# First gated pair by plain products, one fixed order per round, later weight parts, and the squares' adds on VectorE

## The chip, the cores and the metric

The kernel runs on one core of one Trainium2 chip. The metric is the device time of one execution in microseconds. A core has TensorE (matrix products into PSUM), VectorE (DVE in the profile), ScalarE (ACT), GpSimd (POOL) and SyncE (SP, which here issues the loads). All engines run at once and wait for each other by semaphores.

## The reference: two layers of a hybrid decoder block

The input is 512 positions of width 1024, in float32. A layer adds, one after another:

```python
h = h + 0.5 * swiglu(rms_norm(h, ffn1_norm[l]), ffn1_w_gate[l], ffn1_w_up[l], ffn1_w_down[l])
h = h + hybrid_mixer(rms_norm(h, mix_norm[l]), w_in[l], ..., w_out[l])
h = h + 0.5 * swiglu(rms_norm(h, ffn2_norm[l]), ffn2_w_gate[l], ffn2_w_up[l], ffn2_w_down[l])
gate = jax.nn.sigmoid(rms_norm(h, ple_norm[l]) @ ple_w_gate[l])
h = h + gate * (p[l] @ ple_w_proj[l])
```

with `swiglu(x) = (silu(x @ w_gate) * (x @ w_up)) @ w_down` and 2816 hidden columns. `rms_norm` divides by the root of the mean square of a position and multiplies by a gain. The mixer has a recurrent group, a window attention and a gated delta rule side by side, then one output projection. A last `rms_norm` follows the two layers.

## The kernel before, in words

**Layout.** `hT` holds the state transposed: 8 tiles (k) of 128 channels x 512 positions. Every matrix product in float32 is done as three products of a high and a low half (`mm3`): high x high, high x low, low x high. A weight is split by ScalarE (high half, a copy into the rounded format) and VectorE (low half, raw minus high). The rms factor of a position is applied after the product, so the products need only `h` times the gain.

**A norm** (class `Norm`). As soon as a tile k of `hT` is final, `split` makes its high and low halves, and `square` adds its square to `acc` (ScalarE squares; POOL adds for k up to 6, VectorE for the last, L305). `sums` multiplies `acc` by ones on TensorE and takes the inverse root on VectorE (L320 to L334); `rows` spreads it over all partitions (L341, L343).

**A gated block** (`ffn`) has 11 pairs of a gate unit and an up unit ("g", "u"), each of 256 hidden columns, in two rounds of 5 and 6 pairs; behind each round comes its share of the down projection (`down`, tile `pd`). A unit's 1024 x 256 by 1024 x 512 product is done in seven block products (`Unit.p`, numbers 1 to 7) instead of eight, each 12 TensorE products of 256 columns: 84 a unit. For that the operand is combined in advance (`Norm.upper`, `Norm.lower`: differences of quarters of `h`, each split again), and so are the weights (`Weights`): parts a, b, c of 1024 elements and d of 512, two sums `s2` and `s4`, with one raw load summed by a POOL-issued DMA (`load2`, L408). The seven results are added up on VectorE (`c11`, `c21`, `c12`) after copies out of PSUM on ScalarE (L527, L532 `ys`, L536). `Gating` then scales, takes tanh and multiplies.

**Order.** TensorE keeps the order of the program. Other engines' instructions are ordered at compile time by a planner with a cost model, by the order of the program; inside `high_priority` they come ahead, and inside `manual_schedule` ScalarE and VectorE keep the written order among the instructions of that block. Before, a block's first pair (L599 to L650) and the units behind it (L655 to L734) are two such blocks; `taken` places `sums` and `rows` by a count of steps (AT0, AT1).

**Ahead.** `ffn` is a generator. While the stage before it runs, that stage calls `next(ahead)`: first the first raw loads, then part a of unit 0, part a of unit 1, then `s2`, `s4` and d of both and c of unit 0 (L571 to L590). The mixer calls it once ahead of its output projection and at its products n = 0, 2 and 4 (L1473); the embedding (`ple`) calls it at its start and three times behind `rows`, ahead of its gate products (L1508). For the first block of the program the main part calls it between the loads of x (L1567 to L1587). Raw weights share three buffers (tag `wr`).

Of the kernel before, what the change touches and what calls it, by code (L numbers as in the profile page):

```python
# [19 lines left out]
S = 512  # L20
# [23 lines left out]
AT0 = (9, 12)  # L44
# [18 lines left out]
def trunk(ctx: ExitStack, tc: tile.TileContext, a):  # L63
# [168 lines left out]
    class Norm:  # L232
# [32 lines left out]
        def plain(self, k, cs=ALL):  # L265
            x = self.x
            if k < 4:
# [30 lines left out]
        def square(self, k, t512, cs=ALL):  # L298
# [55 lines left out]
    def ffn(l, which, at=AT1):  # L354
        with ExitStack() as es:
# [38 lines left out]
            def load(u):  # L394
                j, m = units[u]
                src = a[f"{m}{which}"][l, j]
                if u not in raw1:
                    raw1[u] = loaded(src[:, 0:8], 8)
                    raw3[u] = wrp.tile([128, 8, 128], F32, tag="wr", name="wr")
# [108 lines left out]

            class Unit:
# [61 lines left out]
            if l + which > 1:  # L571
                for u in range(3):
                    load2(u)
            yield

            for u in range(2):
                load(u)
                load2(u)
                w = pipe[u] = Weights(u)
                w.part("a")  # L580
                yield
            for u in range(2):
                w = pipe[u]
# [3 lines left out]
                if u == 0:  # L587
                    w.part("c")
            load2(2)
# [4 lines left out]
            hs = [[ft.tile([128, 2, S], F32R, name=f"h{i}{c}") for c in "hl"] for i in range(2)]  # L594
            for r, (j0, j1) in enumerate(ROUNDS):
                us = list(range(2 * j0, 2 * j1))
                if r == 0:
                    load(2)
                    with tc.manual_schedule(engines=inner):  # L599
                        g, up = [Unit(*units[u], pipe.pop(u)) for u in us[0:2]]  # L600

                        for qs in (range(3), range(3, 4)):
                            for unit in (g, up):
                                unit.p(2, qs)
                        for i in range(2):
                            taken()
                        w = pipe[2] = Weights(2)
                        g.p(1)
                        taken()
                        g.w.part("b")  # L610
                        g.c11()
                        up.p(1)
                        taken()
                        up.w.part("b")
                        up.c11()
                        g.p(3)
# [1110 lines left out]
```

## Time and profile before

| | |
|---|---|
| time, median of 3 runs | 2096.07 us (2095.33 to 2098.78) |
| the profiled execution's own time | 2096.27 us |
| its span | 2094.3 us, 32231 instructions |
| TensorE busy | 1984.5 us, 12697 products |
| VectorE busy | 1575.2 us, 2578 instructions |
| ScalarE busy | 1000.6 us, 1648 instructions |
| POOL busy | 268.1 us, 254 instructions |
| moved by DMA | 256.08 MB |

A row of the profile names the source line (L305 is line 305), the engine, and out<-in by the program's tile names. Rows that group instructions give their number (x), busy time, mean length and the idle time of the engine ahead of them with what ended it. [...]

### The profile page before, as it was taken

Reading aid. Unit: us, or ns where it says so; the run is one execution under the profiler, and the core shown is the slowest. Engines: PE = TensorE matmul, PEld = TensorE weight load, DVE = VectorE, ACT = ScalarE, POOL = GpSimd, SP = SyncE. Lnnn points to the kernel's source line nnn. Section 1 sums busy time; section 2 is a strip of 40 time slices with the busy share of each in tenths; the row PEclk is TensorE's granted clock in tenths of the full one; section 3 lists DMA queues with packets and bytes.
Section 4 is the critical chain, followed back from the end, with each engine's and each line's share of the span. In section 5 each row is a group of like instructions: output and inputs, shape, how many; then the busy total and the mean of one; then the engine's idle time right before and its main releaser. Section 6 shows DMA issues by size and latency. Waiting matters only on the chain.

```text
span 2094.3 us, 32231 instructions
## 1 busy us (share of the span) xinstructions
PE 1984.5 (95%) x12697; PEld 1767.0 (84%) x12697; DVE 1575.2 (75%) x2578; ACT 1000.6 (48%) x1648; POOL 268.1 (13%) x254
## 2 busy tenths in 40 slices
PE   6999999999989999999979999999899899999997
PEld 5988998777669989997779899988676799899876
DVE  8975983879877857966779569757897888489466
ACT  5542652455645524543546336424365555156343
POOL 3000000152111000002100000010422100000012
PEclk8999999999999999999999999999999999999998
DMA  7763742211045735633337457322112367365411
GB/s 209 194 174 95 187 136 87 89 69 53 19 136 132 198 116 151 169 121 109 113 105 193 125 144 184 121 88 87 59 35 62 106 167 193 89 175 140 140 61 61
DMA packets 85991, 256.08 MB, mean 122 GB/s; under 512 B 9680, under 2 KB 17104, under 8 KB 85584
## 3 DMA queue, kind: packets, MB, share of 16 engines
q1 hardware_dynamic: 73168, 207.89, 31.2%
q0 software_dynamic: 12672, 46.14, 12.5%
q8 instruction: 99, 1.62, 0.3%
q14 instruction: 52, 0.43, 0.1%
HBM read 251.90 MB, written 2.10 MB: 121 GB/s over the span
## 4 chain that ended last, share of the span: by engine, by line
PE 72%; DVE 17%; ACT 4%; DMA 3%; issue 3%; SPq 0%; POOL 0%; DVEq 0%; ACTq 0%
PE pu L469 10%; PE pg L469 10%; PE qu L469 8%; PE qg L469 8%; PE pd L147 7%; PE pd L148 7%; PE pd L149 7%; DMA wr<-in_g_dram 2%; DMA wr<-in_d_dram 1%; PE pp L147 1%; DVE wl L124 1%; PE pp L148 1%; DVE X L252 1%; PE pp L149 1%; PE pwo L149 1%
## 5 line engine op out<-in xcount | busy, mean ns | idle before, releaser
L469 PE MATMUL pu<-T,gh 128*128 128x256 f32 x928 | 169.8, 281 | 0.0
L305 POOL TENSOR_TENSOR acc<-acc,sq 128x512 f32<-128x512 f32 (+1 forms) x55 | 85.5, 1554 | 587.0 <-ACT sq L304 495.0
L437 DVE TENSOR_TENSOR gl<-wr,gh 128x1024 fp32r<-128x1024 f32 x108 | 131.8, 1222 | 36.4 <-ACT gh L432 36.4
L469 PE MATMUL pg<-T,gh 128*128 128x256 f32 x768 | 143.7, 284 | 15.9 <-ACT T L251 7.3
L469 PEld LDWEIGHTS pu<-T,gh 128*128 128x128 f32 x928 | 143.4, 190 | 0.0
L147 PE MATMUL pd<-X,gh 128*128 128x512 f32 x352 | 138.1, 392 | 0.0
L148 PE MATMUL pd<-X,gh 128*128 128x512 f32 x352 | 137.9, 392 | 0.0
L149 PE MATMUL pd<-X,gl 128*128 128x512 f32 x352 | 137.5, 391 | 0.0
L469 PEld LDWEIGHTS pg<-T,gh 128*128 128x128 f32 x768 | 120.5, 192 | 17.7 <-ACT T L251 7.5
L469 PE MATMUL pu<-T,gl 128*128 128x256 f32 x464 | 131.1, 283 | 3.8 <-DVE gl L437 3.8
L129 DVE TENSOR_TENSOR gl<-wr,gh 128x1024 fp32r<-128x1024 f32 x52 | 63.6, 1223 | 94.3 <-ACT gh L128 94.3
L123 ACT ACTIVATE wh<-wr 128x1024 fp32r<-128x1024 f32 (+2 forms) x76 | 77.0, 1013 | 106.8 <-PE pp L148 48.4
L432 ACT ACTIVATE gh<-wr 128x1024 fp32r<-128x1024 f32 x108 | 111.2, 1045 | 28.4 <-PE pd L148 11.0
L469 PE MATMUL pg<-T,wh 128*128 128x256 f32 x640 | 116.8, 281 | 0.0
L128 ACT ACTIVATE gh<-wr 128x1024 fp32r<-128x1024 f32 x52 | 55.2, 1061 | 121.6 <-PE pd L148 95.7
L469 PE MATMUL pg<-T,gl 128*128 128x256 f32 x384 | 109.0, 284 | 1.6 <-DVE gl L437 1.6
L408 POOL DMA_DIRECT2D r<-in_u_dram x44 | 38.5, 875 | 556.9 <-DVE gl L437 179.4
L147 PE MATMUL pp<-X,wh 128*128 128x512 f32 x240 | 102.2, 426 | 0.0
L148 PE MATMUL pp<-X,wh 128*128 128x512 f32 x240 | 98.1, 409 | 3.9 <-DVE X L252 3.9
L437 DVE TENSOR_TENSOR wl<-wr,wh 128x1024 fp32r<-128x1024 f32 x68 | 83.1, 1222 | 24.5 <-ACT wh L432 24.5
L432 ACT ACTIVATE sh<-r 128x512 fp32r<-128x512 f32 x80 | 50.6, 632 | 105.0 <-DVE r L449 105.0
L469 PEld LDWEIGHTS pg<-T,wh 128*128 128x128 f32 x640 | 99.1, 190 | 0.3
(433 smaller groups left out, 6206.5 us busy)
## 6 DMA issues: line engine op xcount, KB each, us to landing
wr<-in_d_dram SPq DMA_DIRECT2D x64, 512.0 KB, 3.7
wr<-in_g_dram SPq DMA_DIRECT2D x44, 512.0 KB, 4.1
r<-in_g_dram SPq DMA_DIRECT2D x44, 512.0 KB, 3.8
wr<-in_u_dram SPq DMA_DIRECT2D x44, 512.0 KB, 3.7
r<-in_u_dram SPq DMA_DIRECT2D x44, 512.0 KB, 3.8
r<-in_g_dram POOLq DMA_DIRECT2D x44, 512.0 KB, 7.2
r<-in_u_dram POOLq DMA_DIRECT2D x44, 512.0 KB, 7.2
wr<-in_wi_dram SPq DMA_DIRECT2D x30, 512.0 KB, 3.3
```

The costliest lines, as they stand in the source:

```text
L123: A.activation(out=hi, in_=raw, func=AF.Copy)
L124: (via or V).tensor_tensor(out=lo, in0=raw, in1=hi.bitcast(F32), op=ALU.subtract)
L128: A.activation(out=hi, in_=x, func=AF.Copy)
L129: V.tensor_tensor(out=lo, in0=x, in1=hi.bitcast(F32), op=ALU.subtract)
L147: T.matmul(out=out, lhsT=wh, rhs=xh, start=start, stop=False)
L148: T.matmul(out=out, lhsT=wh, rhs=xl, start=False, stop=False)
L149: T.matmul(out=out, lhsT=wl, rhs=xh, start=False, stop=stop)
L305: (V if k == KD - 1 else G).tensor_tensor(out=acc, in0=acc, in1=sq, op=ALU.add)
L408: G.dma_start(out=r2.rearrange("p k n -> p (k n)"), in_=src[:, 8:16].rearrange("p k n -> p (k n)"), accum_op=ALU.add)
L432: A.activation(out=self.g[n][0], in_=self.of(n)[0], func=AF.Copy)
L437: V.tensor_tensor(out=g[1], in0=raw, in1=g[0].bitcast(F32), op=ALU.subtract)
L469: T.matmul(out=ps, lhsT=l_[:, q, :], rhs=r_, start=start and q == 0 and i == 0, stop=stop and q == 3 and i == 2, skip_group_check=more)
```

## The change

Seven edits. Only the first block of the program gets the plain pair; the other three blocks keep the seven products, with their orders and weight parts moved.

1. The first pair of the program is done by plain products: `firsts` are the four split raw weights, 24 `mm3` of 512 columns a unit, and the scaling is done from four banks (`PlainGating`). The splits of its norm, its squares and its sums move into that pair's order.
2. The first pair and the units behind it stand in one `manual_schedule` block, and so do the first two chunks of the down weights, in the round's last unit.
3. In the other blocks c of unit 0, and `s2`, `s4` and d of unit 1, are made in the first pair; the calls of `next(ahead)` come later.
4. The raw weights of the mixer's last four output products are loaded a product ahead.
5. The last four weights of the down projection are made ahead of the next norm.
6. Chunks of the down weights lose their high priority.
7. All adds of squares run on VectorE.

```diff
-                (V if k == KD - 1 else G).tensor_tensor(out=acc, in0=acc, in1=sq, op=ALU.add)
+                V.tensor_tensor(out=acc, in0=acc, in1=sq, op=ALU.add)
...
             def grouped(raw, k):
                 w = group(k, 128)
-                with tc.high_priority():
-                    split(raw, *w)
+                split(raw, *w)
...
+            class PlainGating(Gating):
...
+                def scale(self):
+                    self.cg = ft.tile([128, 2, S], F32, tag="cu", name="gs")
+                    for i in range(2):
+                        V.tensor_tensor(out=self.cg[:, i, :], in0=self.ps["g", i], in1=norm.rb, op=ALU.mult)
+                    self.th = ft.tile([128, 2, S], F32, tag="th", name="th")
...
-            if l + which > 1:
-                for u in range(3):
-                    load2(u)
-            yield
-            for u in range(2):
-                load(u)
-                load2(u)
-                w = pipe[u] = Weights(u)
-                w.part("a")
-                yield
-            for u in range(2):
-                w = pipe[u]
-                w.s2()
-                w.s4(0)
-                w.part("d")
-                if u == 0:
-                    w.part("c")
-            load2(2)
+            plain = l + which == 1
+            if plain:
+                raws = {}
+                for m in "gu":
+                    yield
+                    for b in (0, 8):
+                        raws[m, b] = loaded(a[f"{m}{which}"][l, 0][:, b:b + 8], 8)
+                yield
+                firsts = {k: grouped(raw, 8) for k, raw in raws.items()}
+                load(2)
+                load2(2)
+            else:
+                load2(0)
+                load2(1)
+                yield
+                load(0)
+                w = pipe[0] = Weights(0)
+                w.part("a")
+                yield
+                w.s2()
+                w.s4(0)
+                w.part("d")
+                yield
+                load(1)
+                w = pipe[1] = Weights(1)
+                w.part("a")
             yield
...
+            def first_pair():
+                load(2)
+                g, up = [Unit(*units[u], pipe.pop(u)) for u in us[0:2]]
...
+                g.p(1)
+                taken()
+                g.w.part("b")
+                load2(2)
+                g.c11()
+                g.w.part("c")
+                up.p(1)
+                taken()
+                up.w.s2()
+                up.w.s4(0)
+                up.c11()
+                up.w.part("d")
+                g.p(3)
+                taken()
+                g.p(7)
+                taken()
+                up.w.part("b")
...
+            def plain_pair():
+                ps = {}
+                for m in "gu":
+                    for i in range(2):
+                        o = ps[m, i] = bank([128, S], "p" + m)
+                        wh, wl = firsts[m, 8 * i]
+                        for n, (q, j) in enumerate((q, j) for q in range(4) for j in range(2)):
+                            b = 4 * (j if i else 1 - j) + q
+                            xh, xl = (x.both(0, 0, q), x.both(1, 0, q)) if j else (x.first[q][:, 0, :], x.first[q][:, 1, :])
+                            mm3(o, wh[:, b, :], wl[:, b, :], xh, xl, n == 0, n == 7)
+                    if m == "g":
+                        w = pipe[2] = Weights(2)
+                        for q in range(3):
+                            norm.plain(q)
+                            norm.upper(q, x.t512)
+                            norm.lower(q)
+                        for k in range(KD):
+                            norm.square(k, x.t512)
+                        w.part("a")
+                        w.s2()
+                norm.plain(3)
+                norm.upper(3, x.t512)
+                norm.lower(3)
+                norm.sums(t512)
+                w.part("b")
+                w.s4()
+                w.part("d")
+                w.part("c")
+                return None, None, PlainGating(ps, into(0, 0))
...
+                        else:
+                            raws = [loaded(src[l, d][:, t0:t0 + 8, :], 8) for d in range(2)]
                         unit.p(2)
...
                         if w:
                             w.s2()
                             w.lo("b")
+                        else:
+                            made[0] = grouped(raws[0], 8)
                         unit.p(1)
...
+            ws = []
+            for d in range(0, KD, 2):
+                raw = wrp.tile([128, KD, 128], F32, tag="wr", name="wr")
+                for i in range(2):
+                    nc.sync.dma_start(out=raw[:, 4 * i:4 * i + 4, :], in_=src[l, d + i][:, 18:22, :])
+                ws.append(grouped(raw, 8))
             nxt = Norm(gain, False)
...
             for n, d in enumerate(o):
-                if n in (0, 2, 4):
+                if n + 1 in range(4, KD):
+                    raws[n + 1] = wrp.tile([128, KD, 128], F32, tag="wr", name="wr")
+                    nc.sync.dma_start(out=raws[n + 1], in_=a["wo"][l, o[n + 1]])
+                if n == 6:
                     next(ahead)
...
                 nxt.add(d, d5)
+                if n in (3, 4):
+                    next(ahead)
...
             rb = norm.rows()
-            if ahead:
-                for i in range(3):
-                    next(ahead)
...
                     nxt.split(d, t512)
+                    if d in PAIRED[3:5]:
+                        next(ahead)
             ws = [weight(a["pg"][l, d], KD, 128) for d in range(last, KD)]
             if gain is not None:
+                next(ahead)
```

## Rows read from the trace of the kernel before

**Rows 1.** Stages: busy us (x count) of PE, PEld, DVE, ACT, POOL; clock, DMA, GB/s.

```profile
0.00:136.00 136.00, 113.33 (x864) 108.04 (x865) 115.67 (x164) 76.68 (x120) 23.09 (x23) 0.92 0.75 200
192.00:311.00 119.00, 118.60 (x1008) 118.40 (x1007) 101.47 (x125) 68.36 (x98) 6.93 (x8) 1.00 0.60 160
376.70:415.50 38.80, 36.85 (x156) 29.39 (x155) 32.60 (x78) 13.18 (x20) 4.49 (x4) 0.96 0.32 103
576.00:646.00 70.00, 62.50 (x301) 51.16 (x301) 50.93 (x84) 33.40 (x57) 13.45 (x11) 0.93 0.45 124
646.00:742.00 96.00, 91.46 (x754) 90.41 (x754) 81.98 (x110) 52.34 (x76) 6.95 (x9) 0.98 0.70 181
742.00:797.00 55.00, 55.00 (x242) 45.00 (x242) 29.44 (x36) 13.66 (x16) 0.86 (x1) 1.00 0.33 101
981.80:1004.00 22.20, 15.99 (x61) 12.55 (x59) 17.99 (x33) 10.99 (x19) 6.57 (x6) 0.85 0.79 203
1004.00:1050.00 46.00, 45.88 (x219) 38.37 (x218) 37.62 (x55) 23.89 (x40) 7.35 (x5) 0.96 0.29 97
1050.00:1072.00 22.00, 14.03 (x97) 13.53 (x95) 12.33 (x26) 8.75 (x19) 2.90 (x3) 0.77 0.28 72
...
2015.40:2031.30 15.90, 14.24 (x59) 11.33 (x58) 11.13 (x24) 7.56 (x13) 3.47 (x3) 0.89 0.20 65
```

**Rows 2.** Chain of waits, 60 to 80 us: start, length, what.

```profile
62.28 1.69 PE qg L469 x12
...
66.79 1.41 PE pg L469 x12
```

**Rows 3.** TensorE's waits, whole run: total us, times, longest.

```profile
PE pwo L149 <- DVE wl L124: 9.5, 6, 3.3
...
PE pg L469 <- ACT T L251: 7.3, 1, 7.3
...
PE qu L469 <- ACT ys L532: 6.9, 6, 1.9
PE ssc L318 <- DVE acc L305: 5.9, 3, 3.9
...
PE pwo L147 <- ACT wh L123: 5.4, 6, 1.4
```

**Rows 4.** Timeline of VectorE at 1053: start, length, instruction.

```profile
1053.77 2.40 DVE L287 SCALAR_TENSOR_TENSOR t<-hT,par,tg 128x256 f32<-128x256 f32 x1
```

**Rows 5.** Timeline of POOL at 1053.

```profile
1053.71 0.88 POOL L408 DMA_DIRECT2D r<-in_u_dram  x1 [6.38 <-ACT T L251]
1054.32 1.57 POOL L305 TENSOR_TENSOR acc<-acc,sq 128x512 f32<-128x512 f32 x1
```

**Rows 6.** VectorE's instructions by shape, 0 to 70 us: count, busy, mean ns.

```profile
L437 DVE TENSOR_TENSOR gl<-wr,gh 128x1024 fp32r<-128x1024 f32 x6 | 7.3, 1218 | 1.3 <-ACT gh L432 1.3
...
L294 DVE SCALAR_TENSOR_TENSOR t<-hT,neg,t 128x256 f32<-128x256 f32 x4 | 3.8, 952 | 0.0
...
L287 DVE SCALAR_TENSOR_TENSOR t<-hT,par,tg 128x256 f32<-128x256 f32 x4 | 1.9, 477 | 0.0
...
L305 DVE TENSOR_TENSOR acc<-acc,sq 128x512 f32<-128x512 f32 x1 | 0.7, 678 | 0.0
```

**Rows 7.** Timeline of POOL in the last stage.

```profile
2052.20 1.30 POOL L305 TENSOR_TENSOR acc<-acc,sq 128x512 f32<-128x512 f32 x1 [4.26 <-ACT sq L304]
```

**Rows 8.** ScalarE's instructions by shape, 0 to 70 us.

```profile
L128 ACT ACTIVATE T<-t 128x256 fp32r<-128x256 f32 x8 | 3.2, 403 | 2.1 <-DVE t L294 2.1
...
L128 ACT ACTIVATE T<-t 128x512 fp32r<-128x512 f32 x4 | 2.5, 623 | 2.2 <-DVE t L289 2.1
...
L276 ACT ACTIVATE tg<-hT,par 128x256 f32<-128x256 f32 x4 | 2.0, 493 | 0.0
```

**Rows 9.** Timeline of TensorE at 661.

```profile
661.24 0.39 PE L469 MATMUL qg<-T,sl 128*128 128x256 f32 x1 [1.92 <-DVE sl L437]
```

**Rows 10.** Timeline of ScalarE at 736.

```profile
736.47 1.06 ACT L128 ACTIVATE gh<-wr 128x1024 fp32r<-128x1024 f32 x1 [3.58 <-DMA wr<-in_d_dram]
```

More of the change, by code (lines that the diff above doesn't have):

```diff
@@ L266, in plain @@
             x = self.x
-            if k < 4:
+            if k < 4 and hasattr(x, "first"):
+                for i in range(2):
+                    A.activation(out=x(i, "B11", k), in_=x.first[k][:, i, H:S].bitcast(F32), func=AF.Copy)
+            elif k < 4:
                 self.gained(k, HALVES[1], x(0, "B11", k), x(1, "B11", k))
@@ L655, in ffn, with chunk @@
+                t0 = (0, 10)[r]
+                def chunk(d):
+                    if d not in made:
+                        made[d] = grouped(loaded(src[l, d][:, t0:t0 + 8, :], 8), 8)
+                    return made[d]
+                made = {}
                 with tc.manual_schedule(engines=inner):
+                    gate, last, pair, done = None, None, None, True
+                    if r == 0:
+                        gate, last, pair = plain_pair() if plain else first_pair()
+                        us = us[2:]
@@ L698, in ffn @@
                             w.lo("a")
+                        else:
+                            made[1] = grouped(raws[1], 8)
                         unit.p(3)
+                        if pair and not last:
+                            norm.rows()
                         unit.p(7)
@@ L705, in ffn @@
                         if pair:
+                            if not last:
+                                pair.scale()
+                                pair.tanh(0)
+                                pair.tanh(1)
+                                pair.silu()
                             pair.mult()
@@ L745, in end @@
                             ends[e] = halfgroup()
-                            with tc.high_priority():
-                                split(raw, *ends[e])
+                            split(raw, *ends[e])
                         i = 2 * (d % 2)
@@ L766, in ffn @@
                             pipe[2 * j1].whole()
-                        down(pds[d], v, range(8), range(8), True, False)
+                        down(pds[d], chunk(d), range(8), range(8), True, False)
                         if d == 0:
@@ L1571, in t512 @@
     def t512(n):
-        return per.tile([128, S], F32, tag=f"X{next(turn) % KD}", name=n)
-    for i in range(2):
-        load_x(PAIRED[4 * i:4 * i + 4])
-        for k in PAIRED[4 * i:4 * i + 4]:
-            norm.plain(k)
-        if i == 0:
+        return per.tile([128, S], F32, tag=f"X{4 + next(turn) % 4}", name=n)
+    norm.x.t512 = t512
+    norm.x.first = [wide(q) for q in range(4)]
+    load_x(PAIRED[0:2])
+    next(f)
+    load_x(PAIRED[2:8])
+    for q in range(4):
+        norm.gained(q, ALL, norm.x.first[q][:, 0, :], norm.x.first[q][:, 1, :])
+        norm.plain(q + 4)
+        if q == 0:
             next(f)
@@ L1581, in trunk @@
     load_rest()
-    for q in range(4):
-        norm.upper(q, t512)
-        norm.lower(q)
-    next(f)
-    for k in range(KD):
-        norm.square(k, t512)
     def rest(f, norm, gain):
```

123 lines of the change are left out of this document (55 added, 68 removed).

## The prediction

> **What bounds the kernel now.** I read the page's first part, where TensorE is busy nearly all of the span and VectorE comes next; so what can be won is TensorE's idle time and its time at the lower clock level. Then a table of stages [rows 1], which puts that in place; then who made TensorE wait; then single places. A product of 256 columns takes 1.41/12 = 0.1175 us at the full clock [rows 2], one of 512 takes 55.00/242 = 0.227 us (742 to 797, all TensorE [rows 1]). With these, TensorE's need against what each stretch of [rows 1] takes:
>
> (a) 0 to 136, the first round of the program: 10 units of 84 products, 840 x 0.1175 = 98.7 us. Lost: 37.
> (b) 576 to 646, the mixer's output projection and the first eight of the seven-product steps behind it: 192 x 0.227 + 96 x 0.1175 = 55 us, with about 1 for transposes 56. Lost: 14. The second layer has it again.
> (c) 981.8 to 1072, the per-layer embedding and the same eight steps: 240 x 0.227 + 11.3 + 1.5 (sums and rows) = 67.3 us of 90.2. Lost: 23.
> (d) 646 to 742, the rest of a first round: 744 x 0.1175 = 87.4 us of 96. Lost: 8.6, three times in all.
> (e) 376.7 to 415.5, the mixer's start: 1.95 us idle, and a clock of 0.96 that costs 1.6. Lost: 3.5, twice.
> (f) 2015.4 to 2031.3, the second embedding's start: 48 x 0.227 + 1.5 = 12.4 us. Lost: 3.5.
>
> Some 125 us in all. In the steady stretch 192 to 311 nothing is lost and VectorE is busy 101.47 of 119 us, 85% [rows 1]: it catches up 15% there and no more, so a boundary that leaves it late stays late for a while. The waits name it [rows 3]: the projection waits for low halves of weights (L124), the embedding's sums for the sum of squares (L305), the first step for the last split (L251). Two mechanisms lie behind that: weights of the next block are prepared ahead of what is wanted first, and POOL's adds lengthen VectorE's instructions. At 1053.77 an L287 of 128x256 takes 2.40 us beside a POOL add of 1.57 [rows 4, 5]; at the head its mean is 0.477 [rows 6]. That is 1.92 us on the chain that ends in TensorE's wait of 7.3 us [rows 3].
>
> **The squares.** 53 whole adds and two halves go from POOL to VectorE, at 0.678 us each there [rows 6]: 36 us, 4.1 for a norm's six. What comes back lies between 0 (the add at 2052.20 took 1.30 us [rows 7] in the last stage, where VectorE had nothing beside it) and 1.92 us an add (that L287). I take 1.0, nearer to the head, where four L294 average 0.952 against 0.477 [rows 6] and other lines lose too: 6 us a norm. So VectorE's load falls by some 2 us a norm, and the sum of squares no longer trails on an engine that takes 1.3 to 1.6 us an add. If nothing came back, VectorE would carry 36 us more (a rival below).
>
> [...]
>
> **(a) The head.** Before, TensorE runs without a break from 62.28 on; the third unit ends and the fourth begins at 63.97 [rows 2]. TensorE's new work is 96 x 0.227 = 21.8 us against 168 x 0.1175 = 19.7: 2.1 more, hidden as long as VectorE is the late one there. From VectorE go: the parts of two units (each three of 1.218, a half one of 0.68, two sums of 0.68: 5.7, together 11.4), the six sums of their products (3.0 by their sizes), one scaling (1.2), four low halves of B11 (1.9), POOL's lengthening (4). To it come: four low halves of plain weights (4.9), four of whole tiles (2.7), six adds (4.1), scaling and product from four separate banks (1.5) [rows 6]. Net: -21.5 + 13.2 = -8. Against it: the norm's splits and sums now stand inside the fixed order. In each of four rounds VectorE and ScalarE answer each other: ScalarE's 0.49, one of 0.48, high half 0.40, low 0.4, two of 0.48, high 0.62, low 0.68, one of 0.48, high 0.40, low 0.4, and part of the two copies of 0.40 [rows 6, 8]: near 5.8 us a round against 3.4 of VectorE's own work. That is 4 x 2.4 = 9.6 us of standing still at most, and none if the plain splits are placed between. I take 2, since most of those splits are ready then: -6. Ends: -12 (no standing still, every add worth 1.9) and +2. Its DMA is less, four loads of 512 KB instead of 2 x 1792 KB; but the fourth waits for one of three buffers, and in SP's queue behind it stand the third unit's loads and the constants that the norm's sums need. That costs nothing as long as the first plain split ends before TensorE's first 48 products do.
>
> **(b) The output projection.** The first weights' preparation moves from the products n = 0, 2, 4 to n = 3, 4, 6; the raw weights of n = 4 to 7 are loaded a product earlier; c of the first unit, and the sums and d of the second, move into the first pair. The third unit's second load now stands behind part b, whose end frees its buffer before too, so it starts no later. All of this stays inside the stretch, where VectorE is busy 50.93 of 70 us [rows 1]; the load changes by the squares alone, to 49 us, under TensorE's 56. What goes are the waits for L124 and its high halves (9.5 and 5.4 over both layers [rows 3]) and the lower clock behind them; what is late next is the norm's last split, since VectorE has 49 us of work in some 60. Of 14 lost I leave 8.5: -5.5 a layer, -11. Ends -18 and -3.
>
> **(c) The embedding.** In 981.8 to 1004 no weights of the next block are made any more ahead of the sums: 22.2 could become 48 x 0.227 + 1.5 = 12.4, and I take -9. They come in the 46 us of the gate's products instead: VectorE 37.62 [rows 1] + 4.5 (a, two sums, d, a) + 4.1 - 6 = 40 of 46 us, still covered; without that cover the 4.5 would be seen. At 1050 to 1072 the 7.3 us shrink by the 1.9 of that L287 and one queue place, and the clock of 0.77 [rows 1] recovers with them: -4. Sum -13, ends -18 and -5.
>
> **(d) First rounds.** The third unit's part d now stands ahead of the next unit's work; before, TensorE waited 1.92 us for it [rows 9]. The moved c and d can make VectorE up to 2.9 us later just before. I take -1, three times. At the round's end ScalarE stood 3.58 us before a high half whose load had not landed, and behind it the copy-out `ys` held TensorE [rows 10]; six such waits make 6.9 us [rows 3]. The two first chunks now have fixed places, the later ones are still placed by the planner: -2. Together -5, ends -10 and +4. A new wait: the chunk's high half on ScalarE waits for its weight buffer until the previous unit's p5 has run; behind it are c11 and `ys`, and p4 waits for `ys`. p3 and p7 (2.8 us) cover the 2.5 us of ScalarE between.
>
> **(e), (f) Ends of blocks.** No POOL add beside the last splits, and the four last weights made early: -2.5 for each mixer, -3 for the second embedding. Together -8, ends -10.5 and -1.
>
> **Sum.** -6 - 11 - 13 - 5 - 8 = -43 us against the profiled execution's own 2096.27 (its span 2094.3 and 2.0 around it), which is 0.2 above the median shown: 2053.
>
> **The rivals.**
> *Small gain.* VectorE stays what each boundary waits for, in an order no better than now: the head gives 3 and (b) to (f) half, -3 - 18 = -21, 2075. For it: 85% in the steady stretch leaves little to catch up with. Against: in (b) VectorE idles 19 of 70 us.
> *Large gain.* The ends of all parts together: -12 - 18 - 18 - 10 - 10.5 = -68, 2028. For it: TensorE's own need lies 125 us below. Against: each stage still ends in a chain of five or six instructions.
> *Slower.* The adds land on a loaded VectorE and nothing comes back, because what lengthened its instructions was not POOL's add but the DMA descriptors that POOL still writes (an L408 of 0.88 us lay beside the same L287 [rows 5]). Then six adds of 0.68 lie on the path at five places ((a), (b) twice, (c), (f)), 20 us; the moved parts add 2.9 three times, 9; the fixed order costs 2 at the head; against that the 9 of (c): +22, 2118. It decides when VectorE's instructions beside an L408 alone are as long as that L287. Against it: the L294 at the head are long too, and more adds than descriptors ran there.
> *No change.* What the embedding gains, the fixed order loses at the head and in the pairs: 2096.
>
> **How the numbers follow.** Forecast 0.53, small gain 0.21, large gain 0.14, slower 0.08, no change 0.04. About 0.2% (4 us) is what a measurement can tell from no change. Faster: 0.53 + 0.21 + 0.14 = 0.88; same 0.04; slower 0.08. The forecast's own range is 2040 to 2066; with the small gain and the nearer part of the large one, 2030 to 2083 leaves out under 0.2.
>
> **What would show it.** Right: no L305 on POOL, and no L252, L287 or L294 above 1 us; the wait for L305 at the embedding's sums gone, and the first gate product near 994 instead of 1003.7 (less what came before); the program's fourth unit begun at 52 to 60 us; the waits for L124 under 2 us a layer; the 7.3 us down to 3 to 5. Wrong: VectorE idle behind ScalarE for more than 6 us at the head, or the first pair's second half waiting for its parts.

## The result, and the profile after

The changed kernel takes 2064.55 us (median of 4 runs, 2062.52 to 2069.14); the kernel before, on the same chip, 2095.70 (4 runs). The ratio is 0.9853, with an interval of 0.9833 to 0.9874: 31 us faster, where 43 were forecast. 2064.55 lies in the stated range (2030 to 2083) and in the forecast's own (2040 to 2066), 11.6 us above 2053. The profiled execution has a span of 2062.8 us, 31.5 less than before.

The stages, each from the first product of one kind to the first of the next (us, worked out from TensorE's instructions in the two traces):

```
stage                              before    after   difference
head (first round, L0)             135.80   133.79    -2.0
mixer's start, L0 / L1        38.63/38.61  34.99/35.36  -3.6 / -3.3
output projection, L0 / L1    57.97/57.98  47.12/47.10 -10.9 / -10.9
first round behind it, L0/L1 107.69/106.89 111.41/111.15 +3.7 / +4.3
embedding L0: to first gate product 21.89   15.49    -6.4
embedding L0: gate products         45.97   43.89    -2.1
first round behind it, L1          118.46  118.08    -0.4
embedding L1: to first gate product 15.92   15.44    -0.5
```

All second rounds and down projections are unchanged within 0.1 us (but for 0.7 at the first); the rest of the two mixers differs by -0.7 and +1.5. The same stretches in the table by stages of the changed kernel, in the columns of [rows 1] (the clock is TensorE's granted one, a share of full speed and the mean over the stretch; in stretches of 2 us the kernel before shows 1.00 from 4 to 10 us and 0.50 from 12 to 20):

```profile
0.00:133.80 133.80, 115.73 (x792) 104.68 (x793) 107.44 (x159) 75.73 (x120) 9.81 (x15) 0.94 0.68 191
...
374.10:409.10 35.00, 35.00 (x156) 28.28 (x155) 29.28 (x69) 13.75 (x20) 0.00 (x0) 1.00 0.30 107
409.10:568.90 159.80, 150.88 (x925) 119.98 (x923) 136.13 (x393) 92.54 (x232) 49.15 (x48) 0.97 0.13 47
568.90:616.05 47.15, 45.94 (x204) 36.74 (x202) 37.57 (x70) 24.89 (x43) 2.64 (x3) 1.00 0.51 144
616.05:635.80 19.75, 18.47 (x155) 18.00 (x154) 16.98 (x39) 10.21 (x16) 1.71 (x2) 1.00 0.38 109
635.80:727.50 91.70, 85.29 (x698) 84.58 (x697) 76.79 (x94) 50.56 (x74) 6.93 (x8) 0.96 0.72 185
...
967.80:983.24 15.44, 14.24 (x59) 11.31 (x58) 9.83 (x24) 7.66 (x13) 1.73 (x2) 0.89 0.74 185
983.24:1027.10 43.86, 43.86 (x217) 36.95 (x216) 38.64 (x61) 25.99 (x43) 0.86 (x1) 1.00 0.35 113
1027.10:1054.95 27.85, 20.87 (x157) 20.29 (x156) 21.61 (x51) 13.26 (x24) 1.76 (x2) 0.88 0.32 79
...
1420.90:1585.70 164.80, 154.91 (x925) 123.16 (x924) 136.34 (x393) 93.02 (x232) 49.20 (x48) 0.94 0.13 45
```

The first mixer's start runs without a gap at the full clock (38.80 us at 0.96 before, [rows 1]). The projection (568.90 to 616.05) runs at the full clock too, with 1.2 us of gaps and VectorE busy 37.6 of 47.2 us. TensorE's waits, answering to [rows 3]:

```profile
PE pg L475 <- DVE cg L554: 9.8, 3, 3.5
PE qg L475 <- ACT sh L438: 8.6, 1, 8.6
...
PE qu L475 <- ACT ys L558: 7.9, 5, 2.1
...
PE pg L475 <- ACT T L251: 7.5, 3, 6.3
PE qg L475 <- ACT ys L558: 6.9, 8, 2.0
...
PE ssc L321 <- DVE acc L308: 3.3, 4, 1.2
...
PE pwo L147 <- ACT wh L123: 1.4, 2, 0.7
PE pwo L149 <- DVE wl L124: 1.0, 4, 0.3
```

The projection's waits for L124 and L123 went from 9.5 and 5.4 us to 1.0 and 1.4. Two new ones stand on top: 9.8 us for c11 (L554, one in each later first pair), and a single one of 8.6 us in the head, for the high half of the third unit's part d. The wait for the embedding's last split (L251) is 6.3 us, hardly less than the 7.3 of [rows 3].

Squares. Two of VectorE's instructions by shape in the kernel before (count, busy us, mean ns):

```profile
L252 DVE SCALAR_TENSOR_TENSOR X<-hT,par,X 128x512 fp32r<-128x512 f32 x32 | 38.0, 1186 | 4.6 <-ACT X L251 4.6
...
L294 DVE SCALAR_TENSOR_TENSOR t<-hT,neg,t 128x256 f32<-128x256 f32 x16 | 13.0, 815 | 0.0
```

The same, and the adds, in the run of the squares alone (the first experiment below), with its page's line of busy times:

```profile
L305 DVE TENSOR_TENSOR acc<-acc,sq 128x512 f32<-128x512 f32 x60 | 41.3, 689 | 2.9 <-ACT sq L304 2.8
...
L252 DVE SCALAR_TENSOR_TENSOR X<-hT,par,X 128x512 fp32r<-128x512 f32 x32 | 23.9, 748 | 5.3 <-ACT X L251 5.3
...
L294 DVE SCALAR_TENSOR_TENSOR t<-hT,neg,t 128x256 f32<-128x256 f32 x16 | 7.7, 482 | 0.0
```

```profile
PE 1979.7 (95%) x12697; PEld 1763.5 (85%) x12697; DVE 1561.6 (75%) x2633; ACT 999.2 (48%) x1648; POOL 183.5 (9%) x199
```

With 55 more instructions VectorE is busy for *less*: 1561.6 us against 1575.2. Those 55 cost 53 x 0.689 + 2 x 0.423 = 37.4 us, so 37.4 + 13.6 = 51.0 came back, 0.93 us an add.

The trace before shows how. In it 18 `X<-hT,par,X` (own length 0.747 us) began while an add ran on POOL; all of them ended 0.545 to 0.554 us after the add's end, whether they had begun 0.23 or 1.00 us into it. Instructions of two SBUF inputs that began just ahead of an add mostly kept their length, and the add became the longer one: 2.25 us beside a `gl` that began 0.10 ahead of it, against 1.28 at the shortest. The 21 instructions beside an add that read one operand from PSUM (`dt<-pd,rb`, `gs<-ppg,rb` and the like) took 1.00 times their own length.

### The profile page after: what moved, and what is told of

It is laid out like the page before. It is cut to its first block, busy times and chain, and to the rows that moved or that the text cites. A ratio compares the mean times of both kernels' runs of the same rounds, so it can differ in the third digit from the quotient of the medians.

```text
span 2062.8 us, 32001 instructions
## 1 busy us (share of the span) xinstructions
PE 1975.7 (96%) x12625; PEld 1759.0 (85%) x12625; DVE 1555.2 (75%) x2621; ACT 996.1 (48%) x1646; POOL 181.1 (9%) x197
## 4 chain that ended last, share of the span: by engine, by line
PE 77%; DVE 14%; ACT 5%; issue 3%; DMA 1%; POOL 0%; SPq 0%; DVEq 0%; ACTq 0%
PE pu L475 10%; PE pg L475 10%; PE qu L475 8%; PE pd L147 8%; PE pd L149 8%; PE pd L148 8%; PE qg L475 7%; PE pp L147 2%; PE pp L148 2%; PE pp L149 2%; DMA wr<-in_d_dram 1%; PE ppg L149 1%; PE ppg L148 1%; PE ppg L147 1%; DVE gl L443 1%
## 5 line engine op out<-in xcount | busy, mean ns | idle before, releaser
L475 PE MATMUL pu<-T,gh 128*128 128x256 f32 x880 | 159.5, 280 | 0.0
L443 DVE TENSOR_TENSOR gl<-wr,gh 128x1024 fp32r<-128x1024 f32 x102 | 124.6, 1221 | 26.7 <-ACT gh L438 26.7
L123 ACT ACTIVATE wh<-wr 128x1024 fp32r<-128x1024 f32 (+2 forms) x76 | 77.2, 1015 | 133.4 <-PE pp L148 48.6
L475 PEld LDWEIGHTS pu<-T,gh 128*128 128x128 f32 x880 | 134.8, 188 | 0.0
L129 DVE TENSOR_TENSOR gl<-wr,gh 128x1024 fp32r<-128x1024 f32 x53 | 64.3, 1222 | 89.6 <-ACT gh L128 89.6
L147 PE MATMUL pd<-X,gh 128*128 128x512 f32 x328 | 128.8, 393 | 0.0
L149 PE MATMUL pd<-X,gl 128*128 128x512 f32 x328 | 128.4, 391 | 0.0
L148 PE MATMUL pd<-X,gh 128*128 128x512 f32 x328 | 128.1, 391 | 0.0
L475 PE MATMUL pu<-T,gl 128*128 128x256 f32 x440 | 123.2, 280 | 0.0
L475 PE MATMUL pg<-T,wh 128*128 128x256 f32 x592 | 108.3, 281 | 9.8 <-DVE cg L554 9.8
L438 ACT ACTIVATE gh<-wr 128x1024 fp32r<-128x1024 f32 x102 | 105.1, 1046 | 19.6 <-PE pd L148 14.1
L124 DVE TENSOR_TENSOR wl<-wr,wh 128x1024 fp32r<-128x1024 f32 (+2 forms) x64 | 74.1, 1157 | 44.6 <-ACT wh L123 44.3
L438 ACT ACTIVATE sh<-r 128x512 fp32r<-128x512 f32 x80 | 50.7, 633 | 107.8 <-DVE r L455 107.8
L475 PEld LDWEIGHTS pg<-T,wh 128*128 128x128 f32 x592 | 91.3, 189 | 10.7 <-DVE cg L554 10.4
L149 PE MATMUL pp<-X,wl 128*128 128x512 f32 x240 | 97.3, 406 | 1.0 <-DVE wl L124 1.0
```

The lines of the kernel that those rows point to most:

```text
L123: A.activation(out=hi, in_=raw, func=AF.Copy)
L124: (via or V).tensor_tensor(out=lo, in0=raw, in1=hi.bitcast(F32), op=ALU.subtract)
L129: V.tensor_tensor(out=lo, in0=x, in1=hi.bitcast(F32), op=ALU.subtract)
L147: T.matmul(out=out, lhsT=wh, rhs=xh, start=start, stop=False)
L148: T.matmul(out=out, lhsT=wh, rhs=xl, start=False, stop=False)
L149: T.matmul(out=out, lhsT=wl, rhs=xh, start=False, stop=stop)
```

## Experiments

Each was timed against the kernel before on the same chip; the changed kernel's own ratio is 0.9853. Lengths of stages, in us, from the profiled executions, read as above (first rounds in the program's order: behind L0's projection, behind L0's embedding, behind L1's projection; embedding: to its first gate product). In the ten runs with the plain pair and in the changed kernel the head holds a first wait, for the first high half, of 2.3 to 5.0 us, which no edit aims at; differences of about 1 us in the head say nothing.

```
                     ratio [interval]        head  proj. L0/L1  1st rounds L0, L1 x2     embedding L0
squares alone        0.9930 [.9908,.9951]  133.80  57.45/57.95  106.56  113.78  106.58   21.05
squares back         0.9956 [.9933,.9978]  136.88  49.76/49.78  111.09  116.97  110.72   14.29
parts ahead          0.9945 [.9926,.9965]  133.39  57.87/57.59  107.93  117.38  107.97   20.52
seven-product first  0.9887 [.9869,.9906]  140.79  47.08/47.09  110.74  119.07  111.29   13.83
head order           0.9835 [.9815,.9856]  134.93  47.10/47.11  110.80  118.06  110.43   13.84
gate early           0.9845 [.9826,.9864]  133.87  47.11/47.11  109.96  119.85  108.38   13.86
two blocks           0.9810 [.9783,.9836]  136.37  47.11/47.12  108.17  115.59  109.14   15.44
norm free            0.9825 [.9804,.9845]  129.59  47.11/47.09  110.94  117.48  111.11   15.44
free and blocks      0.9784 [.9767,.9800]  128.78  47.09/47.08  108.04  114.75  107.94   15.45
third chunk          0.9836 [.9819,.9854]  132.33  47.10/47.09  109.67  115.24  109.46   13.83
all three            0.9774 [.9755,.9794]  128.12  47.09/47.11  106.59  113.68  106.26   13.83
first part early     0.9774 [.9759,.9789]  128.36  47.09/47.08  106.53  113.49  106.27   16.20
```

**Squares alone.** In the kernel before:

```diff
-                (V if k == KD - 1 else G).tensor_tensor(out=acc, in0=acc, in1=sq, op=ALU.add)
+                V.tensor_tensor(out=acc, in0=acc, in1=sq, op=ALU.add)
```

> The kernel before, and only the adds of the squares moved from POOL to VectorE; nothing else is changed. Theory (a POOL add lengthens the VectorE instructions beside it by about 1 us and trails behind them): faster by 10 to 20 us, near 2080; the mixer's start 38.8 -> 35 to 36 us in each layer, the embedding's wait for the accumulated squares (3.9 us at 987) down to 1.2, the projection 58 -> 55. Rival (the adds only load VectorE, 36 us more, and the whole gain of the change is one of order): 2096 or more, the mixer's start unchanged or longer.

Faster by 0.7% (15 us), 17 in the profiled execution: 3.3 at each mixer's start, 2.0 in the head, 4.7 in the first round behind the embedding. The projection did not move (57.5 and 58.0), and at the embedding TensorE still waited 2.7 us for the squares' sum: two low halves of the next block's weights, 2.4 us of VectorE, stood ahead of the last adds. So the squares alone are worth half of the change; at the projection and the embedding's start the order is what counts.

**Squares back.** The same line of the changed kernel turned back.

> The changed kernel with the adds of the squares on POOL again. Theory: slower by 10 to 20 us, near 2080, if the adds and the order gain each for themselves; the mixer's start back from 35 to 38.8 us, the projection from 47.2 to 50 or more. Rival (only the order counts): 2065 or less.

Slower than the changed kernel by 1.0% (0.9956 against 0.9853), some 21 us, at the upper end of the theory; 12 us in the profiled execution, which was the shortest of the seven. The mixer's starts are 40.8 and 37.0, the projections 49.8: with parts made late the projection keeps 8.2 of its 10.9 us beside POOL's adds, and the squares bring the other 2.7. In the other order, alone, they brought next to nothing there.

**Parts ahead.**

```diff
-                load(0)
-                w = pipe[0] = Weights(0)
-                w.part("a")
-                yield
-                w.s2()
...
+                for u in range(2):
+                    load(u)
+                    w = pipe[u] = Weights(u)
+                    w.part("a")
+                    yield
+                for u in range(2):
+                    w = pipe[u]
+                    w.s2()
+                    w.s4(0)
+                    w.part("d")
+                    if u == 0:
+                        w.part("c")
...
-                if n == 6:
+                if n in (0, 2, 4):
                     next(ahead)
```

> The changed kernel with the preparation of the next block's weights as before: all parts made in the stage ahead, at the old places of the projection's and the embedding's loops, and the projection's own weights loaded when they are wanted; adds on VectorE, first round and head as changed. Theory (order alone is worth about as much as the squares): projection 47.2 -> 53 or more in each layer, the embedding up to its first gate product 15.4 -> 20, first rounds 91.5 -> 88: sum +10 to +18, near 2079. Rival (what the projection gains is given back in the first round behind it, since VectorE makes the same parts there): within 4 us of 2065.

Slower by 0.9%. The projections are back at 57.9 and 57.6, the embedding's start at 20.5; TensorE waits 8.6 us for L124 again. First rounds fall by 3.5, 0.7 and 3.2. So the late preparation, together with the projection's own weights loaded a product ahead (no run parts the two), wins 10.6 in a projection and gives back a third of it in the round behind.

```profile
568.81:626.68 57.87, 50.55 (x203) 39.54 (x202) 43.06 (x78) 27.00 (x46) 2.64 (x3) 0.91 0.48 133
626.68:734.61 107.93, 101.32 (x852) 100.42 (x851) 88.81 (x123) 58.67 (x86) 8.64 (x10) 1.00 0.67 169
```

VectorE carries 43.1 us here in the projection against 37.6 in the changed kernel, and 88.8 in the first round against 17.0 + 76.8 = 93.8: 5 to 5.5 us have crossed the boundary.

**Seven-product first pair.** The program's first pair, its parts and its norm as before, inside the one order of the round:

```diff
-            plain = l + which == 1
-            if plain:
+            head = l + which == 1
+            plain = False
+            if head:
```

> The changed kernel with the program's first pair by the seven-product steps again, its norm outside the fixed order and its parts made ahead, as before. Theory (the plain pair starts TensorE sooner but gives most of it back in an 8.6 us wait for the third unit's part d): slower by 2 to 4 us, near 2068. By the forecast's own term for the head (-6): 2071. Rival (the plain pair costs more than it gives, because the norm stands in the fixed order): 2062 or less.

Slower by 0.34%, 7 us, where the theory said 2 to 4 and the forecast's term for the head 6. Its head takes 140.8 us. But the same steps as a block of their own take 133.8 (squares alone). So the plain pair gains 7 us inside the new order of the round, and nothing against the old head with the squares moved. A wait of 4.1 us for c11 stands in this head, as in the changed kernel's later first pairs, and none in the head of the squares alone; that the one block is to blame, and not the places of the chunks or of the sums, is not shown for the head.

**Head order.**

```diff
                 norm.plain(3)
+                w.part("b")
+                w.s4()
+                w.part("d")
                 norm.upper(3, x.t512)
                 norm.lower(3)
                 norm.sums(t512)
-                w.part("b")
-                w.s4()
-                w.part("d")
...
                         unit.p(3)
-                        if pair and not last:
-                            norm.rows()
                         unit.p(7)
+                        if pair and not last:
+                            norm.rows()
```

> The changed kernel, head only: the third unit's part b, its sum and its part d stand ahead of the norm's last round of splits and of the sums' chain of small instructions, and the rows' products one step later. Theory (the 8.6 us wait is made by the order alone: VectorE spends 4 us on the last splits and 4 on the chain first): the wait down to 1 to 4 us, the head 133.8 -> 129 to 131, total 2060. Rival (VectorE is late by its load, so the wait comes back at the rows or at the fourth unit): head within 1 us of 133.8, 2064.

The 8.6 us wait went, and came back at the next places. TensorE's waits up to 140 us:

```profile
PE pg L147 <- ACT gh L128: 3.7, 1, 3.7
PE prow L344 <- DVE rl L333: 3.7, 1, 3.7
PE qu L475 <- ACT ys L558: 3.1, 2, 1.9
PE pg L475 <- DVE cg L554: 2.4, 1, 2.4
```

The head is 134.9, or 133.6 but for the first wait, which is 3.7 here and 2.4 in the changed kernel. The rival was right: what is put first in a fixed order only changed who waits.

**Gate early.**

```diff
                 up.p16()
+                pair = Gating(g.c, up.c, into(0, 0))
+                pair.scale()
+                pair.tanh(0)
+                pair.tanh(1)
                 w.s4()
                 w.part("d")
...
                         unit.c11()
+                        if soon:
+                            w.s2()
+                            w.lo("b")
```

> The changed kernel; in the three first pairs by seven products the gate's scaling and tanh are moved forward, ahead of the third unit's sum and part d, and the fourth unit's sum and low half b go behind c11 of the third. Theory (the new waits of 3.1 to 3.5 us for c11 come from VectorE standing 1.2 us behind the tanh and from silu, sum and low half queued ahead of c11): those waits under 1.5 us, first rounds 111.3 -> 108 in each mixer's FFN and 118.1 -> 115, total 2056. Rival (VectorE's load is the bound and the wait only moves to the next unit): first rounds within 1 us, 2064.

The wait for c11 fell from 9.8 to 3.3 us over three places, but the one of `qg` for `ys` rose from 6.9 to 13.7:

```profile
PE qg L475 <- ACT ys L558: 13.7, 8, 3.9
...
PE pg L475 <- DVE cg L554: 3.3, 3, 1.1
```

First rounds are -1.5, +1.8 and -2.8, the time 0.08% less, inside the interval. The wait moved, as the rival said, though single rounds moved by more than its 1 us.

**Two blocks.**

```diff
                         gate, last, pair = plain_pair() if plain else first_pair()
                         us = us[2:]
+                with tc.manual_schedule(engines=inner):
                     for u in us:
```

> The changed kernel with the first pair and the rest of the round as two ordered blocks again, so that the planner may interleave them; nothing else is changed. Theory (one fixed order for the whole round is what makes first rounds longer, by 1.4 to 3.6 us each as the earlier runs suggest): first rounds -1.5 to -4 each, total 2054 to 2060. Rival (it is the work moved into the first pair, 2.9 us, and not the order): first rounds within 1 us, 2064.

First rounds shorter by 3.2, 2.5 and 2.0, the head longer by 2.6; ratio 0.9810. So the single order lengthens the later first rounds, by 7.7 us over the three. It is not alone: parts ahead, with the single order kept and the c11 wait still there (9.2 us), took 7.4 off the same three. The squares alone, which have neither, stand 13.7 below the changed kernel there, so the two nearly add up. Of the 7.7 us only 2.2 are less waiting; 5.5 are TensorE's own busy time, which fell from 103.7, 105.1 and 103.9 us to 101.6, 103.7 and 101.8 while the granted clock rose from 0.97 to 1.00 in the first and the third. VectorE's load did not fall (93.7 and 93.3 us in the first). VectorE's timeline in the changed kernel shows how (start, length, instruction, idle time before it and what ended it):

```profile
640.39 0.68 DVE L568 TENSOR_TENSOR cu<-pu,ys 128x512 f32<-128x512 f32 x1
641.00 1.22 DVE L443 TENSOR_TENSOR wl<-wr,wh 128x1024 fp32r<-128x1024 f32 x1
642.13 1.22 DVE L496 TENSOR_TENSOR cg<-cg,rb 128x1024 f32<-128x1024 f32 x1
644.56 1.23 DVE L503 SCALAR_TENSOR_TENSOR th<-th,cg 128x1024 f32<-128x1024 f32 x1 [1.22 <-ACT th L500]
645.71 0.69 DVE L449 TENSOR_TENSOR wr<-r,wr 128x512 f32<-128x512 f32 x1
646.31 1.22 DVE L443 TENSOR_TENSOR gl<-r,gh 128x1024 fp32r<-128x1024 f32 x1
647.44 0.41 DVE L554 TENSOR_TENSOR cg<-cg,pg 128x256 f32<-128x256 f32 x1
```

and in the kernel of two blocks:

```profile
642.95 1.22 DVE L496 TENSOR_TENSOR cg<-cg,rb 128x1024 f32<-128x1024 f32 x1
644.09 0.69 DVE L455 TENSOR_TENSOR r<-wr 128x512 f32<-128x512 f32 x1
645.39 1.22 DVE L503 SCALAR_TENSOR_TENSOR th<-th,cg 128x1024 f32<-128x1024 f32 x1 [0.62 <-ACT th L500]
```

In one order the gate's scaling stands behind the pair's last low half, VectorE idles 1.22 us for the tanh, and c11 (L554), for which TensorE waits, comes four instructions later. With two blocks the planner slips the gate's scaling and silu in ahead of the pair's own last sums, puts a sum of weights (L455) behind the scaling, and VectorE idles 0.62 us.

**Norm free.** The head's splits and squares outside the order, and so the third unit's b, sum and d ahead of the sums' chain, as in the run of the head's order:

```diff
-                        for q in range(3):
-                            norm.plain(q)
-                            norm.upper(q, x.t512)
-                            norm.lower(q)
-                        for k in range(KD):
-                            norm.square(k, x.t512)
                         w.part("a")
...
     load_rest()
+    for q in range(4):
+        norm.plain(q)
+        norm.upper(q, t512)
+        norm.lower(q)
+    for k in range(KD):
+        norm.square(k, t512)
```

> The changed kernel, head only: the norm's splits and squares stand outside the fixed order, as in the kernel before, while the plain pair stays. Theory (VectorE stands 7.3 of 29.9 us in 18.8 to 48.7 because splits answer ScalarE one by one in a fixed order): the standing falls by 3 or more, the 8.6 us wait to under 6, the head 133.8 -> 130, total 2061. Rival (the planner puts splits ahead of the plain weights' low halves and TensorE's first products wait): head 134 or more, 2064 to 2070.

Head 129.6 us, 4.2 shorter; the 8.6 us wait is gone and one of 4.7 for the squares stands in its place. VectorE's standing in 18.8 to 48.7 fell only from 29.9 - 22.6 = 7.3 to 29.9 - 23.6 = 6.3 us, less than the 3 that I expected. Over the first 60 us its standing behind ScalarE fell more, from 12.8 to 9.2. Putting first what TensorE needs next was not enough by itself (head order); with the splits free as well it was.

**Free and blocks.** The last two edits, the second in the three later first pairs only.

> The changed kernel with two edits that each gained alone: the head's norm outside the fixed order (head 129.6 there), and in the three later first pairs by seven products the pair and the rest of the round as two ordered blocks (first rounds 108.2, 115.6, 109.1 there). Theory (they act at different places and add): head 130, first rounds 108, 115.5, 109, total 2064.5 - 4.2 - 7.7 = 2052. Rival (the planner's freedom at the one place undoes the other, as the head lost 2.6 with two blocks): 2058 or more.

They add: head 128.8, first rounds 108.0, 114.8, 107.9; 2050.08 us.

**Third chunk.** ScalarE before the end of a first round of the changed kernel:

```profile
717.44 1.05 ACT L128 ACTIVATE gh<-wr 128x1024 fp32r<-128x1024 f32 x1
722.41 1.06 ACT L128 ACTIVATE gh<-wr 128x1024 fp32r<-128x1024 f32 x1 [3.92 <-DMA wr<-in_d_dram]
723.37 0.61 ACT L128 ACTIVATE sh<-wr 128x512 fp32r<-128x512 f32 x1
723.89 0.58 ACT L558 ACTIVATE ys<-qu 128x512 f32<-128x512 f32 x1
```

The third chunk's split, placed by the planner, waits 3.9 us for its load, with `ys` behind it.

```diff
                         unit.p(4)
                         unit.c21()
+                        if not w and r == 0:
+                            chunk(2)
+                            half_ends(0)
```

> The changed kernel; at the end of each first round the split of the third chunk of the second product's weights, and of the first half group behind it, get a fixed place behind the last unit's copy-out, instead of one that the planner chooses. Theory (the waits of 0.9 to 2.1 us near the end of each first round, 6 us over the four, are ScalarE standing 3.9 us before that third chunk's load with the copy-out queued behind it): those waits under 0.4, each first round shorter by 0.9 to 2, total 2059. Rival (the load is late anyway, so the following product waits as long as the copy-out did): 2064.

The copy-out now comes first and waits for TensorE alone:

```profile
720.50 1.05 ACT L128 ACTIVATE gh<-wr 128x1024 fp32r<-128x1024 f32 x1
724.46 0.60 ACT L558 ACTIVATE ys<-qu 128x512 f32<-128x512 f32 x1 [2.91 <-PE qu L475]
725.88 0.38 ACT L562 ACTIVATE e<-pu 128x256 f32<-128x256 f32 x1 [0.82 <-PE pu L475]
726.16 1.05 ACT L128 ACTIVATE gh<-wr 128x1024 fp32r<-128x1024 f32 x1
```

First rounds are 1.5, 1.7, 2.8 and 1.7 us shorter (head included); the down projections behind give back 0.7, 0.3, 0 and 1.6. The time, 0.9836, is 0.17% below the changed kernel's, which the intervals do not part; the waits do.

**All three.**

> The changed kernel with the three edits that gained: the head's norm outside the fixed order, two ordered blocks in the later first rounds, fixed places for the third chunk and the first half group at each first round's end. Theory (three places, so the gains add): 2050 - 5 = 2045, the last waits of the first rounds gone. Rival (with freer placing the planner finds the load late elsewhere): 2049 or more.

2047.36 us, ratio 0.9774: 47 us under the kernel before and 17 under the changed one, the best version found. Its first rounds are 106.6, 113.7 and 106.3, as short as with the squares alone, though the down projections behind them are 0.5 to 2.1 us longer; against free and blocks the two intervals overlap.

**First part early.**

```diff
             rb = norm.rows()
+            if ahead:
+                next(ahead)
```

> The kernel of the run beside this one, and in the first embedding one of the three preparation steps (part a of the first unit, 1.2 us of VectorE) made ahead of the gate products, where VectorE is busy 9.8 of 15.4 us, instead of among them, where it is busy 38.6 of 43.9. Theory (VectorE's load in the gate stage is what makes the 6.3 us wait for the last split): that wait down to 5, the embedding's start unchanged, total 1 us less than beside it. Rival (even one part ahead of the sums delays them, as three did by 5 us): first gate product 1.5 to 2 us later, wait unchanged, total 1 to 2 us more.

The first gate product comes 16.20 us after the stage's start instead of 13.83; 1.6 of these go with the granted clock (0.89 against 1.00, and at 0.89 the other kernels take 15.44), 0.8 remain. The wait for the last split falls from 6.0 to 5.7, and the time is the same. Neither theory is borne out: 0.8 us lost ahead and 0.3 gained behind are less than the times can part.

## Why the prediction was right, and where it was not

**The squares: right.** By themselves they took 13.6 us off VectorE, where 2 us a norm, 18 over nine norms, were forecast, and an add was worth 0.93 us against my 1.0. No L305 is left on POOL, and in the changed kernel no L252 exceeds 0.76 us and no L290 or L297 (before: L287, L294) 0.49. The 18 `X` that an add lengthened read two SBUF inputs (all 32 `X` averaged 1.186 us, with the squares alone 0.748); the 21 instructions beside an add that read one operand from PSUM kept their length (1.00 times). A whole add (84.6 us less of POOL's busy time over 55, 1.54 each) does not come back: most of the instructions that began just ahead of an add kept their length. The rival "slower" rested on POOL's DMA instructions (L408, 0.88 us each, which it took for the writing of descriptors) doing the lengthening: beside an L408 alone, 170 VectorE instructions of the kernel before took 0.999 of their median length with the squares alone, on average, and beside a POOL add alone 100 took 1.67. It is refuted.

**(a) Head: -2.0 against -6.** The fourth unit begins at 58.7 instead of 64.0, inside my 52 to 60, but 3 us are lost again behind it. I took 2 us for the fixed order's standing still, with 9.6 as the most. VectorE stood 7.3 us between 18.8 and 48.7 (2.9 before), 5.5 of them behind ScalarE; over the first 60 us it stood 12.8 us behind ScalarE (5.6 before), past the 6 that I named as proof against me. The runs show more: moving the splits out gives 4.2 back, and inside the new order a seven-product head takes 7 us more. That (a) counted the plain pair as a gain over the old head was wrong as the change has it; with its norm free it is one of 4 to 5 (133.8 with the squares alone, 129.6 and 128.8 free).

**(b) Projection: -10.9 twice against -5.5 twice.** The mechanism was right (waits for L124 1.0 us in all, under 2 a layer as forecast), the size too small: of the 14 us I took 5.5 and left 8.5, because VectorE would have 49 us of work in some 60. That load came as forecast, 48.8 us in the 60.7 from the projection's first product to the end of the eighth step, but only 37.6 of it fell in the projection's 47.1, and it did not hold TensorE there. What had held it was in part the order on ScalarE. Before (all engines):

```profile
590.28 1.06 ACT L432 ACTIVATE gh<-wr 128x1024 fp32r<-128x1024 f32 x1 [5.21 <-DMA wr<-in_g_dram]
591.25 0.83 ACT L123 ACTIVATE wh<-wr 128x768 fp32r<-128x768 f32 x1
...
592.13 0.51 PE L147 MATMUL pwo<-X,wh 128*128 128x512 f32 x1 [1.18 <-ACT wh L123]
```

The high half for the next block stood 5.2 us before its load, and the projection's own high half, whose raw weights had been asked for before 528, stood behind it. The granted clock gave another part: TensorE's busy time in the projection fell from 50.7 us at 0.91 (the line below, before) to 45.9 at 1.00, 4.8 of the 10.9 us.

```profile
575.90:633.90 58.00, 50.69 (x203) 39.55 (x203) 44.72 (x72) 27.43 (x46) 11.73 (x9) 0.91 0.47 132
```

**(d) First rounds: +3.7, +4.3 and -0.4, where -5 in all was forecast.** This is the step that failed, with its sign. I had priced d's place and the chunks, and taken the 2.9 us that c and d move as small. The squares by themselves shortened the three rounds by 6.1 us; the rest of the change then lengthened them by 13.7. Two things did it: 5 us more VectorE work in a stretch where it is 84% busy (parts ahead: -7.4 over the three rounds), which I had put at nearly nothing, and the single order with its new wait for c11 (two blocks: -7.7), for which I had no term outside the head. The -2 for the chunks did not come either: the waits for `ys` near the ends are 6.0 us before and after, because only two of the three splits got fixed places; with the third fixed (third chunk) all four are gone, and the down projections take part of the gain back.

**(c) Embedding: -8.5, against -13.** The wait for the squares' sum went from 3.9 to 1.2 and the first gate product comes 6.4 us sooner, not 9. At the last split 6.3 us stay. From 1024.8 to 1036.8 VectorE works without a pause:

```profile
1033.50 0.48 DVE L292 SCALAR_TENSOR_TENSOR t<-hT,neg,t 128x256 f32<-128x256 f32 x1
1033.90 0.42 DVE L129 TENSOR_TENSOR T<-t,T 128x256 fp32r<-128x256 f32 x1
1034.23 0.42 DVE L1619 TENSOR_TENSOR hT<-hT,gs 128x256 f32<-128x256 f32 x1
```

The slow L287 of [rows 4] is gone (L290 takes 0.48), but VectorE's queue is full. The squares by themselves had brought this wait to 5.0 us, as forecast, and it is 5.0 with parts ahead too (5.5 with the squares back); with the parts among the gate's products it is 6.3. Taking one part out again gave only 0.3 (first part early), so how much of the wait is VectorE's load stays open.

**(e), (f): -7.4 against -8.** The two mixers' starts gave 6.9. The second embedding's start gave 0.5, at a granted clock of 0.89; at 1.00 it took 13.83 us in the run of the squares alone, which is 2.1 less than before.

So (b) was 10.8 better than forecast, (d) 12.6 worse, (c) 4.5, (a) 4 and (e), (f) 0.6 worse. The prediction had counted the first eight steps of a round to (b) and (c); counted so, (b) is -19.5 instead of -11, (c) -9.9 instead of -13 and (d) +6.8 instead of -5, the same picture. The total came near by luck, because two misses cancelled.

## What to carry to other kernels

Take the next stage's weight preparation out of a stage whose own splits wait behind it, but count what arrives behind the boundary: here a third came back at once. Look for a split that stands in an engine's queue ahead of its load: here ScalarE stood 5.2 us behind one in the projection and 3.9 us at a round's end. A written-out order pays where the planner puts the wrong thing first (the third chunk), and costs where it forbids filling a wait with the neighbouring block's work; keep blocks short. An add on POOL is not free if it lengthens VectorE's instructions: moving 55 adds onto the busier engine lowered that engine's own load (1575.2 to 1561.6 us).

## What was not expected of the hardware

The mixers' middle stretch has the same 925 or 926 products in all kernels, and VectorE's work in it is alike (136 to 138 us), yet it took 159.8 us at a mean granted clock of 0.97 and 164.8 at 0.94 in one and the same execution (409.1 and 1420.9 in the table above). Over the 14 profiled executions it lay between 159.9 and 164.9. So 5 us a layer, a sixth of the whole gain, come and go with the clock in a stretch that no edit is aimed at; stages have to be compared, not only totals. What decides between the two stays open.
